# Gate matrices of a dense expert layer as three bf16 products instead of one fp32 product, and 18 more score blocks computed ahead of the expert stream

## The chip, the cores and the metric

The kernel runs as one program on one core of a Trainium2 chip. The metric is the time of one execution on the device in microseconds (us), the median of the runs. A core has TensorE (PE in the profile; its weight loads are listed as PEld), VectorE (DVE), ScalarE (ACT), GpSimd (POOL), SyncE (SP, which here only issues transfers), and 16 DMA engines.

## The reference, cut to what matters

Two transformer blocks follow one another on 512 tokens of width 1024. Each ends in a mixture of 16384 single-row experts, and only that part is touched. For a token, 8 heads choose 16 experts each, which makes 128 slots of an expert number and a gate.

```python
e   = e1 * 128 + e2                 # [tokens, 8, 16] expert numbers
g   = softmax(top)                  # gates
act = gelu(einsum('thkd,td->thk', u_tab[e], x))
y   = einsum('thk,thkd->td', g * act, v_tab[e])
```

## The kernel before, in words

`peer` is called once in each block. It treats tokens in two ways. For 128 of the 512 tokens it gathers the chosen rows of both tables by indirect DMAs (the events `g_u`, `g_v`). For the other 384 tokens (NDT) it computes densely: all 16384 experts are taken as 128 blocks of 128, and block e has three parts.

- **The score block** (`emit_A`): `a_dma` loads 512 KB of the first table (tile `ur`, line 1094); `a_hi` rounds it on ACT (`uh`, line 1099); `a_lo` takes the rest on GpSimd (`ul`, line 1105); `a_mm` makes 24 matmuls of 384 columns (tile `pa`, lines 1112, 1113 and 1115) and a Gelu on ACT into a tile `ga` (line 1117). There are NA = 28 tiles `ga`, and two buffers each of `ur`, `uh` and `ul`.
- **The gates**: for each token a 128 x 128 matrix that holds the gate of expert 128 a + b at [b, a]. The 384 matrices go to DRAM (`Gd`) and come back four expert blocks at a time (`gbuf`, line 1258).
- **The output** (`y`, lines 1293 to 1295): scores times gates (`w`, `wh`, `wl`) with the second table's block (`vr`, `vh`, `vl`), 18 matmuls of 512 columns into six accumulators.

The order of a call is as follows. **Routing** finds experts and gates (written out by hand, with score blocks 0 to 18 between its steps). Then comes the **gate loop**: 12 groups (`tg`) of 32 tokens, each in four steps of 8 tokens. A step makes the one-hot rows `oh2` of the second index on DVE (line 1198) and `oh1`, the one-hot rows of the first index times the gate, on GpSimd or for every fourth step on DVE (line 1200). PE makes one fp32 product for each token (line 1206), whose two operands are read at a stride of 8 elements of 4 bytes; the trace lists each such product as two loads and two matmuls. ACT copies four tokens at a time out of PSUM (`stg`, line 1208), and SP writes each group to `Gd`. `run_ahead` puts three score blocks ahead of the loop, one behind each of the groups in RG, and the rest up to 28 behind the loop. Then comes the **stream** over the 128 blocks: block e makes the output of e and the score block of e + NA, and spreads the gather events evenly over the blocks up to 99.

Outside of the routing and of GpSimd's work in the stream the scheduler of the language sets the order of instructions on each engine; each engine then works in that order, and so does SP's queue of transfers.

## Time and profile before

| what | us |
|---|---|
| median of 3 runs | 4092.33 |
| lowest and highest run | 4079.37, 4106.96 |
| span of the profiled execution | 4090.4 |
| gate loop, first block of the model | 752.6 to 954.4 |
| stream, first block of the model: first and last output matmul | 970.6 to 1959.9 |
| gate loop, second block | 2899.5 to 3100.2 |
| stream, second block | 3116.4 to 4081.1 |

The median lies 1.9 us above the profiled span. The two gate loops and the two streams make up most of the program. A row of a table by stretches gives for each engine its busy time and, after an x, its number of instructions. PE's matmuls overlap, so the pace of matmuls is read from start to start, or from the length of a row of many, and not from the duration of one.

### The profile page before, as it was taken

What the parts mean: (1) busy time and instruction counts of PE and PEld (TensorE: products, weight loads), DVE (VectorE), ACT (ScalarE), POOL (GpSimd) and SP (SyncE); (2) the same over time, 40 slices, a digit from 0 to 9 for tenths busy, and PEclk for the clock granted to TensorE, in tenths of its full rate; (3) what the DMA queues carried; (4) which work ended last, traced back from release to release, by engine and by line L of the source; (5) the groups of instructions that cost most, each with busy time, mean ns of one, the idle gap of its engine ahead of it and who ended that gap; (6) DMA issues with size and microseconds to landing.
All of it is one profiled execution on the core that took longest, in us unless ns stands there. A gap on an engine that the chain in (4) does not pass through costs nothing. (4 is left out here: it accounts for less than half of the span.)

```text
span 4090.4 us, 53234 instructions
## 1 busy us (share of the span) xinstructions
PE 3876.8 (95%) x19062; PEld 3370.2 (82%) x19062; DVE 3004.6 (73%) x5440; ACT 1654.8 (40%) x2567; POOL 2145.8 (52%) x1353
## 2 busy tenths in 40 slices
...
GB/s 112 99 111 106 52 113 79 101 134 230 302 319 320 315 311 315 318 275 221 90 81 57 93 75 100 102 114 79 98 134 250 299 322 314 311 306 308 299 254 150
DMA packets 330057, 784.31 MB, mean 192 GB/s; under 512 B 32048, under 2 KB 148864, under 8 KB 326400
## 3 DMA queue, kind: packets, MB, share of 16 engines
...
q14 instruction: 115, 0.94, 0.1%
...
## 5 line engine op out<-in xcount | busy, mean ns | idle before, releaser
L1105 POOL TENSOR_TENSOR ul<-ur,uh 128x1024 fp32r<-128x1024 f32 x256 | 676.5, 2643 | 378.0 <-ACT uh L1099 259.5
L1112 PE MATMUL pa<-phi,uh 128*128 128x384 f32 x2048 | 695.5, 340 | 0.8 <-ACT ga L1117 0.8
L1113 PE MATMUL pa<-plo,uh 128*128 128x384 f32 x2048 | 694.8, 339 | 0.0
L1294 PE MATMUL y<-vl,wh 128*128 128x512 f32 x1536 | 606.2, 395 | 26.1 <-DVE vl L1263 22.4
L1295 PE MATMUL y<-vh,wl 128*128 128x512 f32 x1536 | 609.2, 397 | 11.3 <-DVE wl L1269 11.3
L1293 PE MATMUL y<-vh,wh 128*128 128x512 f32 x1536 | 603.8, 394 | 1.3 <-ACT wh L1268 1.2
L1243 DVE SCALAR_TENSOR_TENSOR acc<-vrow,act,acc 128x1024 f32<-128x1024 f32 x256 | 392.3, 1532 | 196.6 <-DMA vrow<-in_expert_v_dram,ei 99.5
L1230 DVE SCALAR_TENSOR_TENSOR urow<-urow,hgat 128x1024 f32<-128x1024 f32 x256 | 392.0, 1534 | 172.0 <-DMA urow<-in_peer_u_dram,ei 85.5
L1268 ACT CAST wh<-w 128x384 fp32r<-128x384 f32 x256 | 131.2, 513 | 736.0 <-PE y L1294 483.8
L1099 ACT CAST uh<-ur 128x1024 fp32r<-128x1024 f32 x256 | 269.3, 1052 | 382.9 <-PE pa L1113 149.2
L1115 PE MATMUL pa<-phi,ul 128*128 128x384 f32 x2048 | 402.5, 339 | 18.0 <-POOL ul L1105 17.9
L1112 PEld LDWEIGHTS pa<-phi,uh 128*128 128x128 f32 x2048 | 389.0, 190 | 10.0 <-ACT ga L1117 1.1
L1113 PEld LDWEIGHTS pa<-plo,uh 128*128 128x128 f32 x2048 | 389.1, 190 | 9.6
L1263 DVE TENSOR_TENSOR vl<-vr,vh 128x1024 fp32r<-128x1024 f32 x236 | 353.4, 1498 | 34.6 <-DMA ur<-in_peer_uT_dram 16.2
L1115 PEld LDWEIGHTS pa<-phi,ul 128*128 128x128 f32 x2048 | 362.0, 190 | 19.9 <-POOL ul L1105 19.9
L1206 PE MATMUL pgg<-oh,oh 128*128 128x128 f32 x1536 | 374.3, 421 | 4.4 <-DVE oh L1198 3.9
L1206 PEld LDWEIGHTS pgg<-oh,oh 128*128 128x128 f32 x1536 | 369.9, 337 | 7.1 <-issue 5.3
L1294 PEld LDWEIGHTS y<-vl,wh 128*128 128x128 f32 x1536 | 290.5, 189 | 93.5 <-DVE vl L1263 32.3
L1295 PEld LDWEIGHTS y<-vh,wl 128*128 128x128 f32 x1536 | 290.5, 189 | 85.0 <-DVE wl L1269 22.5
L1293 PEld LDWEIGHTS y<-vh,wh 128*128 128x128 f32 x1536 | 290.8, 189 | 55.5 <-ACT wh L1268 1.7
L77 DVE TENSOR_TENSOR wl<-wr,wh 128x512 fp32r<-128x512 f32 (+1 forms) x276 | 198.9, 729 | 148.9 <-ACT wh L76 148.8
L1200 POOL TENSOR_TENSOR oh<-oha,ohb 128x1024 f32<-128x1024 f32 x72 | 218.2, 3033 | 143.9 <-PE pgg L1206 104.5
...
## 6 DMA issues: line engine op xcount, KB each, us to landing
vr<-in_peer_v_dram SPq DMA_DIRECT2D x128, 512.0 KB
ur<-in_peer_uT_dram SPq DMA_DIRECT2D x128, 512.0 KB
vr<-in_expert_v_dram SPq DMA_DIRECT2D x128, 512.0 KB
ur<-in_expert_uT_dram SPq DMA_DIRECT2D x128, 512.0 KB
...
wr<-in_w_in_dram SPq DMA_DIRECT2D x104, 256.0 KB
...
```

The costliest lines, as they stand in the source:

```text
L1099: A.copy(out=uh, in_=ua[e])
L1105: G.tensor_tensor(out=ul, in0=raw, in1=uh.bitcast(F32), op=OP.subtract)
L1112: T.matmul(pa, uh[:, k, :], hi[:, k, 0:NDT], start=(k == 0), stop=False)
L1113: T.matmul(pa, uh[:, k, :], lo[:, k, 0:NDT], start=False, stop=False)
L1115: T.matmul(pa, ul[:, k, :], hi[:, k, 0:NDT], start=False, stop=(k == 7))
L1206: T.matmul(pg[:, j, :], oh2[:, :, 4 * q + j], oh1[:, :, 4 * q + j], start=True, stop=True)
L1230: V.scalar_tensor_tensor(out=row, in0=row, scalar=1.0, in1=hg_, op0=OP.mult, op1=OP.mult, accum_out=act[:, k:k + 1])
L1243: V.scalar_tensor_tensor(out=acc, in0=vrow.pop(k - 2), scalar=act[:, k - 2:k - 1], in1=acc, op0=OP.mult, op1=OP.add)
L1263: (G if side and EV <= e < EW else V).tensor_tensor(out=vl, in0=vr, in1=vh.bitcast(F32), op=OP.subtract)
L1293: T.matmul(y[t][c], wh[:, ts], vh[:, cs_], start=(e_ == 0), stop=False)
L1294: T.matmul(y[t][c], wh[:, ts], vl[:, cs_], start=False, stop=False)
L1295: T.matmul(y[t][c], wl[:, ts], vh[:, cs_], start=False, stop=(e_ == 127))
```

## The change: what it does, and the diff

In the gate loop the gate is split into three bf16 parts whose sum is the fp32 gate. `oh2` becomes a contiguous bf16 row of 128 for each token, made by eight small DVE comparisons a step. The first index is no longer taken apart: one comparison of 1024 elements gives its one-hot rows (tile `oh12`), and three multiplications give the rows times each part. These tiles are laid out so that a token's operand is 64 pairs of neighbouring bf16 numbers. PE makes three products for each token, each with a weight load of its own. GpSimd has no work left in the loop.

NA goes from 28 to 30. Of the later score blocks every sixth (35, 41, ... 125: 16 blocks) is also computed in the gate loop: its `ga` is written to DRAM (`gad`, 196.6 KB) by SP and read back in the stream, where the score block is then left out. The list `todo` has 27 blocks: three stand ahead of the loop, 24 in it, two a group. For them `a_lo` runs on DVE instead of GpSimd. The diff, without removed comments and docstrings:

```diff
-    O1 = 3
...
-    GM = 4
-    GR = 3
     TB = 3
-    NA = 28
+    NA = 30
...
     TG = 32
+    TK = 8
+    RP = 2
+    SP = 6
     NTG = NDT // TG
...
-        def a_lo(e):
+        def a_lo(e, eng=G):
             raw, uh = ua[e]
             ul = ub.tile([128, 8, 128], F32R, name="ul", tag="ul")
-            G.tensor_tensor(out=ul, in0=raw, in1=uh.bitcast(F32), op=OP.subtract)
+            eng.tensor_tensor(out=ul, in0=raw, in1=uh.bitcast(F32), op=OP.subtract)
             ua[e] = (uh, ul)
-        def a_mm(e):
+        def a_mm(e, keep=None):
             uh, ul = ua.pop(e)
             pa = psA.tile([128, NDT], F32, name="pa", tag="pa")
             for k in range(8):
                 T.matmul(pa, uh[:, k, :], lo[:, k, 0:NDT], start=False, stop=False)
             for k in range(8):
                 T.matmul(pa, ul[:, k, :], hi[:, k, 0:NDT], start=False, stop=(k == 7))
-            ga = ub.tile([128, NDT], F32, name="ga", tag="ga", bufs=NA)
+            ga = keep.tile([128, NDT], F32, name="gs", tag="gs") if keep else ub.tile([128, NDT], F32, name="ga", tag="ga", bufs=NA)
             A.activation(out=ga, in_=pa, func=AF.Gelu)
-            gas[e] = ga
-
-        def emit_A(e):
+            if keep:
+                S.dma_start(out=gad[e], in_=ga)
+            else:
+                gas[e] = ga
+
+        def emit_A(e, eng=G, keep=None):
             a_dma(e)
             a_hi(e)
-            a_lo(e)
-            a_mm(e)
+            a_lo(e, eng)
+            a_mm(e, keep)
         gas = {}
...
-        def run_ahead(n):
-            for e in range(len(gas), min(NA, len(gas) + n)):
-                emit_A(e)
-
-        E = rr.tile([128, 4, 128], F32, name="E")
+        gad = {e: dram.tile([128, NDT], F32, name=f"gad{nm}{e}") for e in range(NA + SP - 1, 128, SP)}
+        todo = list(range(16 + TA, NA)) + list(gad)
+        def run_ahead(n, keep):
+            for _ in range(min(n, len(todo))):
+                e = todo.pop(0)
+                emit_A(e, V, keep if e in gad else None)
         rwx = ExitStack()
         rw = rwx.enter_context(tc.tile_pool(name=nm + "rw", bufs=2))
+        E = rw.tile([128, 4, 128], F32, name="E", bufs=1)
...
+        V.tensor_copy(out=ei, in_=E)
         rwx.close()
         qpx.close()
         rp = ExitStack()
         r1 = rp.enter_context(tc.tile_pool(name=nm + "r1", bufs=1))
-        V.tensor_copy(out=ei, in_=E)
-        iota = r1.tile([128, 128], F32, name="iota")
-        S.dma_start(out=iota, in_=I["k_iota"])
+        s2 = r1.tile([128, NDT], F32, name="s2")
+        io2 = r1.tile([128, 128], BF16, name="io2")
+        sD = [r1.tile([128, NDT * RP], BF16, name=f"sD{j}") for j in range(4)]
         ix = ExitStack()
         ixp = ix.enter_context(tc.tile_pool(name=nm + "ix", bufs=1))
-        i1 = ixp.tile([128, 3, ND, 128], I32, name="i1")
-        f12 = ixp.tile([128, 3, ND, 128], F32, name="f12")
-        V.tensor_scalar(out=i1[:, 0], in0=ei[:, 0:ND, :], scalar1=11, scalar2=None, op0=OP.logical_shift_right)
-        V.tensor_scalar(out=i1[:, 1], in0=ei[:, 0:ND, :], scalar1=7, scalar2=15, op0=OP.logical_shift_right, op1=OP.bitwise_and)
-        V.tensor_scalar(out=i1[:, 2], in0=ei[:, 0:ND, :], scalar1=127, scalar2=None, op0=OP.bitwise_and)
-        sT = [r1.tile([128, NDT], F32 if j == 3 else BF16, name=f"sT{j}") for j in range(4)]
-        for j in range(4):
-            if j < 3:
+        iota = ixp.tile([128, 128], F32, name="iota")
+        S.dma_start(out=iota, in_=I["k_iota"])
+        i1 = ixp.tile([128, 2, ND, 128], I32, name="i1")
+        f12 = ixp.tile([128, 2, ND, 128], F32, name="f12")
+        V.tensor_scalar(out=i1[:, 0], in0=ei[:, 0:ND, :], scalar1=7, scalar2=None, op0=OP.logical_shift_right)
+        V.tensor_scalar(out=i1[:, 1], in0=ei[:, 0:ND, :], scalar1=127, scalar2=None, op0=OP.bitwise_and)
+        def spread(j, src):
+            A.copy(out=sD[j].rearrange("p (t r) -> p t r", r=RP), in_=src.unsqueeze(2).broadcast_to([128, NDT, RP]))
+        for j in range(3):
+            if j < 2:
                 A.copy(out=f12[:, j], in_=i1[:, j])
             pt = (pst, pss)[j // 2].tile([128, 4, 128], F32, name="ptE", tag=("tr", "sc")[j // 2])
             for t in range(ND):
-                T.transpose(pt[:, t, :], GT[:, t, :] if j == 3 else f12[:, j, t, :], ident)
-            A.copy(out=sT[j], in_=pt[:, 0:ND, :].rearrange("p a b -> p (a b)"))
+                T.transpose(pt[:, t, :], GT[:, t, :] if j == 2 else f12[:, j, t, :], ident)
+            pf = pt[:, 0:ND, :].rearrange("p a b -> p (a b)")
+            if j == 0:
+                spread(0, pf)
+                continue
+            if j == 1:
+                A.copy(out=s2, in_=pf)
+                continue
+            for i in range(3):
+                part = ixp.tile([128, NDT], BF16, name=f"gpart{i}")
+                V.tensor_copy(out=part, in_=pf)
+                if i < 2:
+                    rest = ixp.tile([128, NDT], F32, name=f"grest{i}")
+                    V.tensor_tensor(out=rest, in0=pf, in1=part, op=OP.subtract)
+                    pf = rest
+                spread(1 + i, part)
+        irep = r1.tile([128, 128 // RP, TK * RP], BF16, name="irep")
+        V.tensor_copy(out=irep.rearrange("p g (t i) -> p g t i", i=RP),
+                      in_=iota.rearrange("p (g i) -> p g i", i=RP).unsqueeze(2).broadcast_to([128, 128 // RP, TK, RP]))
+        V.tensor_copy(out=io2, in_=iota)
         ix.close()
-        run_ahead(TB)
+        gsp = rp.enter_context(tc.tile_pool(name=nm + "gs", bufs=2))
+        run_ahead(TB, gsp)
         rw = rp.enter_context(tc.tile_pool(name=nm + "gg", bufs=2))
-        irep = r1.tile([128, 128, 8], BF16, name="irep")
-        V.tensor_copy(out=irep, in_=iota.unsqueeze(2).broadcast_to([128, 128, 8]))
-        irtg = r1.tile([128, 16, TG], BF16, name="irtg")
-        V.tensor_copy(out=irtg, in_=iota[:, 0:16].unsqueeze(2).broadcast_to([128, 16, TG]))
+        def onehot(name, in0, j, c0, op, o=None):
+            if o is None:
+                o = rw.tile([128, 128 // RP, TK * RP], BF16, name=name, tag=name)
+            V.tensor_tensor(out=o, in0=in0, in1=sD[j][:, c0 * RP:(c0 + TK) * RP].unsqueeze(1).broadcast_to([128, 128 // RP, TK * RP]), op=op)
+            return o
         for tg in range(NTG):
             stg = rw.tile([128, 128, TG], F32, name="stg", tag="stg")
-
-            def row(j, c0, n, m):
-                return sT[j][:, c0:c0 + n].unsqueeze(1).broadcast_to([128, m, n])
-
             c0 = tg * TG
-            oa_ = rw.tile([128, 8, TG], F32, name="oha", tag="oha")
-            V.tensor_tensor(out=oa_, in0=irtg[:, 0:8], in1=row(0, c0, TG, 8), op=OP.is_equal)
-            V.tensor_tensor(out=oa_, in0=oa_, in1=row(3, c0, TG, 8), op=OP.mult)
-            ob_ = rw.tile([128, 16, TG], F32, name="ohb", tag="ohb")
-            V.tensor_tensor(out=ob_, in0=irtg, in1=row(1, c0, TG, 16), op=OP.is_equal)
-            for t8 in range(TG // 8):
-                tk = slice(t8 * 8, t8 * 8 + 8)
-                oh2 = rw.tile([128, 128, 8], F32, name="oh2", tag="oh2")
-                V.tensor_tensor(out=oh2, in0=irep, in1=row(2, c0 + t8 * 8, 8, 128), op=OP.is_equal)
-                oh1 = rw.tile([128, 128, 8], F32, name="oh1", tag="oh1", bufs=O1)
-                (V if (tg * 4 + t8) % GM == GR else G).tensor_tensor(
-                    out=oh1.rearrange("p (a b) t -> p a b t", a=8), in0=oa_[:, :, tk].unsqueeze(2).broadcast_to([128, 8, 16, 8]),
-                    in1=ob_[:, :, tk].unsqueeze(1).broadcast_to([128, 8, 16, 8]), op=OP.mult)
-                for q in range(2):
+            for tk0 in range(0, TG, TK):
+                oh2 = rw.tile([128, TK, 128], BF16, name="oh2", tag="oh2")
+                for i in range(TK):
+                    V.tensor_scalar(out=oh2[:, i], in0=io2, scalar1=s2[:, c0 + tk0 + i:c0 + tk0 + i + 1], scalar2=None, op0=OP.is_equal)
+                eq1 = onehot("oh12", irep, 0, c0 + tk0, OP.is_equal)
+                oh1 = [onehot(f"oh1{j}", eq1, 1 + j, c0 + tk0, OP.mult, eq1 if j == 2 else None) for j in range(3)]
+                for q in range(TK // 4):
                     pg = psm.tile([128, 4, 128], F32, name="pgg", tag="mm")
-                    for j in range(4):
-                        T.matmul(pg[:, j, :], oh2[:, :, 4 * q + j], oh1[:, :, 4 * q + j], start=True, stop=True)
-                    ts = t8 * 8 + 4 * q
+                    for i in range(4):
+                        for j in range(3):
+                            T.matmul(pg[:, i, :], oh2[:, 4 * q + i], oh1[j][:, :, (4 * q + i) * RP:(4 * q + i + 1) * RP], start=(j == 0), stop=(j == 2))
+                    ts = tk0 + 4 * q
                     A.copy(out=stg[:, :, ts:ts + 4].rearrange("p e t -> p t e"), in_=pg)
             S.dma_start(out=Gd[0][:, tg], in_=stg[:, 0:G0])
             S.dma_start(out=Gd[1][:, tg], in_=stg[:, G0:])
-            if tg in RG:
-                run_ahead(1)
+            run_ahead(-(-len(todo) // (NTG - tg)), gsp)
+        rp.close()
         vrs = {e: load_v(e) for e in range(2)}
-        rp.close()
         pctx.close()
-        run_ahead(NA)
...
             with tc.manual_schedule(engines={mybir.EngineType.Pool}):
-                if e + NA < 128:
+                if e + NA in gad:
+                    gas[e + NA] = ub.tile([128, NDT], F32, name="ga", tag="ga", bufs=NA)
+                    S.dma_start(out=gas[e + NA], in_=gad[e + NA])
+                elif e + NA < 128:
                     emit_A(e + NA)
```

How the rows stand now: first PE at the start of the gate loop, where `pgg` is the gate matrix in PSUM, `pa` a score block, and the operands of `pgg` are the moving and the stationary one. Before:

```order
L1115 MATMUL pa_7174<-phi_4498,ul_7172 128x384 x8
L1206 MATMUL pgg_7218<-oh1_7216,oh2_7214 128x128 x4
L1206 MATMUL pgg_7224<-oh1_7216,oh2_7214 128x128 x4
L1206 MATMUL pgg_7234<-oh1_7232,oh2_7230 128x128 x4
L1206 MATMUL pgg_7240<-oh1_7232,oh2_7230 128x128 x4
```

and now:

```order
L1115 MATMUL pa_7203<-phi_4498,ul_7201 128x384 x8
L1228 LDWEIGHTS oh2_7234
L1228 MATMUL pgg_7250<-oh10_7245,oh2_7234 128x128
L1228 LDWEIGHTS oh2_7234
L1228 MATMUL pgg_7264<-oh10_7245,oh2_7234 128x128
L1112 MATMUL pa_7418<-phi_4498,uh_7414 128x384
L1113 MATMUL pa_7418<-plo_4499,uh_7414 128x384
L1228 LDWEIGHTS oh2_7234
L1228 MATMUL pgg_7250<-oh11_7247,oh2_7234 128x128
```

Eight products a step became 24 pairs of load and product, and the matmuls of a score block stand among them.

Then DVE in the same place. Before, one step after another:

```order
L1198 TENSOR_TENSOR oh2_7246<-irep_7204,sT2_7076 128x1024
L1200 TENSOR_TENSOR oh1_7264<-oha_7209,ohb_7212 128x1024
L1198 TENSOR_TENSOR oh2_7262<-irep_7204,sT2_7076 128x1024
L1191 TENSOR_TENSOR oha_7353<-irtg_7206,sT0_7074 128x256
L1198 TENSOR_TENSOR oh2_7286<-irep_7204,sT2_7076 128x1024
```

and now:

```order
L1221 TENSOR_SCALAR oh2_7322<-io2_7081,s2_7080 128x128 x6
L1212 TENSOR_TENSOR oh12_7331<-irep_7124,sD0_7082 128x1024
L1105 TENSOR_TENSOR ul_7449<-ur_7445,uh_7447 128x1024
L1212 TENSOR_TENSOR oh10_7333<-oh12_7331,sD1_7083 128x1024
L1212 TENSOR_TENSOR oh11_7335<-oh12_7331,sD2_7084 128x1024
L1221 TENSOR_SCALAR oh2_7366<-io2_7081,s2_7080 128x128
L1212 TENSOR_TENSOR oh12_7331<-oh12_7331,sD3_7085 128x1024
```

A step has four operations of 1024 and eight of 128, and on every second step a subtraction of a score block stands among them.

Last SP's queue in the stream near the first score block that comes back from DRAM. Before:

```order
L1131 DMA vr_8654<-in_peer_v_dram 128x1024
L1094 DMA ur_8740<-in_peer_uT_dram 128x1024
L1131 DMA vr_8726<-in_peer_v_dram 128x1024
L1094 DMA ur_8815<-in_peer_uT_dram 128x1024
L1131 DMA vr_8801<-in_peer_v_dram 128x1024
```

and now:

```order
L1094 DMA ur_10780<-in_peer_uT_dram 128x1024
L1134 DMA vr_10690<-in_peer_v_dram 128x1024
L1293 DMA ga_10588<-gad135_4924 128x384
L1094 DMA ur_10852<-in_peer_uT_dram 128x1024
L1278 DMA gbuf_11029<-Gd11_4810 128x12x128
```

The load of `ga` stands behind a load of the second table and ahead of the next load of the first one.

## Rows read from the trace of the kernel before

**Rows 1.** The page: span, then busy us (share) xinstructions by engine.

```profile
span 4090.4 us, 53234 instructions
PE 3876.8 (95%) x19062; PEld 3370.2 (82%) x19062; DVE 3004.6 (73%) x5440; ACT 1654.8 (40%) x2567; POOL 2145.8 (52%) x1353
```

**Rows 2.** Stretches: us, busy (x) of PE, PEld, DVE, ACT, POOL; PEclk, DMA share, GB/s.

```profile
752.60:954.40 201.80, 199.29 (x844) 197.70 (x843) 152.92 (x89) 103.55 (x104) 118.65 (x40) 0.98 0.32 128
2899.50:3100.20 200.70, 198.83 (x844) 197.64 (x844) 152.83 (x90) 104.13 (x104) 116.32 (x40) 0.99 0.32 130
955.00:970.00 15.00, 15.00 (x88) 15.00 (x87) 4.15 (x4) 6.90 (x9) 8.50 (x5) 1.00 0.81 279
1400.00:1500.00 100.00, 100.00 (x508) 91.07 (x508) 81.26 (x86) 35.81 (x49) 76.38 (x44) 1.00 0.88 314
```

**Rows 3.** Gate product's tile, first block: duration ns min/median/max, first and last start.

```profile
L1206 PE MATMUL pgg<-oh,oh x768: 415/420/578, 752.8 to 953.8; 128*128 128x128 f32 x192
L1208 ACT COPY stg<-pgg x96: 1012/1026/1136, 754.9 to 954.3; 128x512 f32<-128x512 f32 x96
```

**Rows 4.** Who waited for that tile: us, times.

```profile
  ACT stg L1208: 93.7, 96
  DVE oh L1198: 41.3, 19
```

**Rows 5.** PE by time in the gate loop: start us, us, instruction, xcount.

```profile
893.74 14.07 PE L1206 MATMUL pgg<-oh,oh 128*128 128x128 f32 x58
```

**Rows 6.** PE by time in the routing: score block, contiguous fp32 product of 128.

```profile
606.05 0.34 PE L1113 MATMUL pa<-plo,uh 128*128 128x384 f32 x1
606.22 1.55 PE L1115 MATMUL pa<-phi,ul 128*128 128x384 f32 x8
607.61 1.05 PE L910 MATMUL psc<-keysT,qs 128*128 128x128 f32 x8
```

**Rows 7.** The tile of that contiguous product: duration ns min/median/max, first and last start.

```profile
L910 PE MATMUL psc<-keysT,qs x256: 270/275/422, 537.6 to 2846.7; 128*128 128x128 f32 x128
```

**Rows 8.** PE's weight loads by time, products of only 64 columns.

```profile
2111.06 1.42 PEld L1521 LDWEIGHTS dpo<-va,dpT 128*128 128x128 f32 x12
2112.40 0.19 PEld L119 LDWEIGHTS mm<-wl,phi 128*128 128x128 f32 x1
```

**Rows 9.** DVE by time in the routing: bf16 comparison of 800, then next operation.

```profile
605.02 1.05 DVE L960 TENSOR_TENSOR eq<-crep,fpos 128x800 bf16<-128x800 bf16 x2
605.99 0.48 DVE L919 MAX8 vals<-scs 128x8 f32<-128x128 f32 x2
```

**Rows 10.** DVE by time: a small operation with a constant, then the next.

```profile
2720.05 0.27 DVE L925 FIND_INDEX8 idx<-vals,scs 128x8 uint32<-128x128 f32 x1
2720.25 0.06 DVE L925 MATCH_VALUE_LOAD idx<-vals,scs 128x8 f32 x1
2721.82 0.16 DVE L938 TENSOR_SCALAR fidx<-idx 128x64 f32<-128x64 uint32 x1
2721.92 0.20 DVE L939 CAST fidx<-idx 128x64 f32<-128x64 uint32 x1
```

**Rows 11.** DVE by time in the gate loop: two fp32 operations without GpSimd.

```profile
907.86 1.23 DVE L1198 TENSOR_TENSOR oh<-irep,sT 128x1024 f32<-128x1024 bf16 x1
909.00 1.22 DVE L1200 TENSOR_TENSOR oh<-oha,ohb 128x1024 f32<-128x1024 f32 x1
```

**Rows 12.** Groups of instructions (count, busy us, mean ns): ACT's part of a score block.

```profile
L1099 ACT CAST uh<-ur 128x1024 fp32r<-128x1024 f32 x256 | 269.3, 1052 | 382.9 <-PE pa L1113 149.2 <-DMA ur<-in_expert_uT_dram 89.3 <-DMA ur<-in_peer_uT_dram 76.7
L1117 ACT ACTIVATE ga<-pa 128x384 f32<-128x384 f32 x256 | 125.4, 490 | 175.3 <-PE pa L1115 173.0 <-issue 2.0
```

**Rows 13.** DVE by time between loop and stream, first block.

```profile
969.12 1.38 DVE L1267 TENSOR_TENSOR w<-gbuf,ga 128x384 f32<-128x384 f32 x2 [1.77 <-DMA gbuf<-Gd]
```

**Rows 14.** DVE's waits in the first stream: us in total, times, longest.

```profile
DVE acc L1243 <- DMA vrow<-in_peer_v_dram,ei: 94.8, 38, 6.1
```

**Rows 15.** The waits of SP's queue in the first stream.

```profile
SPq L1131 <- DVE vl L1263: 632.7, 101, 11.0
```

3 lines of the change are left out of this document (removed).

## The prediction

> **What bounds the kernel now.** I read the page's shares first [rows 1]: PE is busy for 95% of the span, no other engine for more than 73%. Time can therefore only come from less PE work, or from PE's few gaps. Then I read the two stages that the change touches in the table by stretches [rows 2]. In the gate loop of the first block PE is busy for 199.3 of 201.8 us, with DMA at a share of 0.32. In a dense piece of the stream PE is busy for 100 of 100 us, DVE for 81, POOL for 76, and the DMA engines have a share of 0.88 at 314 GB/s. PE sets both stages; in the stream DMA comes next, in the gate loop nothing is near.
>
> In the gate loop a token is one fp32 product, which runs as two matmul instructions: 768 for 384 tokens [rows 3]. 58 of them stand in one row of 14.07 us [rows 5]; without the overlap of the last one that is (14.07 - 0.42) / 57 = 0.239 us each, 0.479 us a token, 184 us a block of the model. Three score blocks stand in the same window (844 - 768 = 76 matmuls, [rows 2]). Theirs start (1.55 - 0.34) / 7 = 0.173 us apart [rows 6], so a score block is 24 x 0.173 = 4.15 us and three are 12.5. 184 + 12.5 is 196.5 of the 201.8 us. ACT and DVE wait for these products (93.7 and 41.3 us, [rows 4]), not the other way round. Why the product is dear is in the rows too: a product of the same shape whose operands lie contiguously takes (1.05 - 0.275) / 7 = 0.111 us an instruction [rows 6, 7], less than half.
>
> In the stream 508 matmuls in 100 us [rows 2] at 42 a block (24 + 18) are 8.27 us a block; taking 4.15 off leaves 4.12 us for the output part.
>
> **The change part by part.** The sum is made for one model block and doubled; the second block shows the same loop (200.7 us, [rows 2]).
>
> *Moved score blocks: -79 us.* Before, PE has done 29 score blocks when the first output matmul starts (19 in the routing, three ahead of the loop, three in it, four behind it), and 99 are left for the stream. Now 48 are done (19 + 27, and blocks 30 and 31 behind the loop), and 80 are left. The stream sheds 19 x 4.15 = 79 us of PE work. This alone saves nothing: 24 of them now stand in the loop, where three stood, and are charged there.
>
> *The loop on PE.* A step of 8 tokens has 24 products of one pass, and on average half a score block (24 in 48 steps), 2.08 us. No row has a bf16 product. Bound from below: 0.055 us, half of the contiguous instruction [rows 6, 7], which streams its 128 columns twice. Bound from above: 0.12 us, half of today's strided instruction [rows 5]; the products of 64 columns, which wait for their weight loads, give (1.42 - 0.19) / 11 = 0.112 us a load of 128 fp32 columns [rows 8], and every new product has a load of its own. The weights are now contiguous, the moving operand is read in pairs, and a bf16 column has half of the bytes, so the row that it is nearest to lies between these; I take the middle of 0.055 and 0.112, 0.084 us. A step is then 24 x 0.084 + 2.08 = 4.09 us, the loop's 48 steps 197 us.
>
> On this price the Trainium skill has two rules, both in "TensorE: Matmul & The Clock Gate". Its section on LDWEIGHTS counts columns, not bytes: 128 / 1.2 = 107 ns a load, which agrees with the 0.112 us of [rows 8] and speaks against my middle value; by it a step would be 4.65 us and the loop 223. Its section on the back-to-back issue gap gives about 81 ns for a stream of pairs of load and matmul of 128 columns, which would make 193 us.
>
> *The loop on DVE.* Four operations of 1024 bf16 elements: the routing's bf16 comparison of 800, with the same kind of broadcast, takes (605.99 - 605.02) / 2 = 0.485 us [rows 9], two elements a cycle with a rest of some 0.07; scaled, 0.60 us. Eight comparisons of 128 with a constant: at most 0.20 us (a search over 128 at one element a cycle, 2720.05 to 2720.25), at least 0.06 (the smallest operation there), and I take 0.10, the step from the 64-element operation to the next [rows 10]. Half a subtraction of a score block, 1.14 us alone [rows 11]: 0.57. Sum 2.40 + 0.80 + 0.57 = 3.8 us a step, 181 us; with the upper bound 4.6 us, 219. These use undisturbed prices, since POOL has nothing left in the loop. So DVE is just behind PE, and as each of a step's first products waits for one DVE tile and the tiles have two buffers, I add 5% for the two waiting for each other: 207 us. ACT has two copies (2 x 1.03, [rows 3]) and half of 1.05 + 0.49 [rows 12], 2.8 us a step, and is hidden; it is next if both others fall. So the loop with 24 score blocks takes 207 us, 5 more than today with three.
>
> *The setup.* Transposes, splitting and copies of the gate's parts stand ahead of the loop, beside the 12.5 us of three score blocks as now. DVE's three subtractions are new there. I charge 3 us; PE's three blocks are the cover, and without them some 8 us would show.
>
> *Between loop and stream.* Today 16.8 us pass from the last gate product (953.8, [rows 3]) to the first output matmul (970.6, in the table of stages); the row of w [rows 13] waits for the gates' return from DRAM. PE is filled then, 15.00 of 15.00 us [rows 2], by four score blocks; now it has the two and idles for 8 us. The chain through DRAM is the same, so the time between the two stays; no row shows what PE needs to pick up again, and between 0 and the 8 us of idle I allow 2.
>
> *Transfers in the stream.* A block moves 314 GB/s x 8.27 us = 2.60 MB. One in six now drops 524 KB and reads 197 KB: 6 x 2.60 - 0.33 = 15.3 MB in 5 x 8.27 + 4.12 = 45.5 us, 336 GB/s, a share of 0.94. DVE waits for gathered rows already (94.8 us for those of the second table alone, [rows 14]), and its 6.7 us a block (81 of 100) must fit in 7.6. Bound below: 0, PE stays the bound. Above: 314 GB/s is all there is; then 15.3 MB take 48.7 us, 3.2 more for each of 16 groups, 51 us. I take 12, near the lower end, since a share of 0.88 is not yet full. The load of `ga` waits on SP's queue for `w` of its block; behind it stands the next load of the first table. SP already stands 632.7 us waiting for `vl` of the same blocks [rows 15], so I charge nothing; if that load came late, `uh` and then PE's next score block would wait.
>
> *Sum.* -79 + 5 + 3 + 2 + 12 = -57 us a block, -114 in all. The profiled span would go from 4090.4 to 3976; the median lies 1.9 above its span: **3978 us**.
>
> **The rivals.**
>
> *A. Each product pays its weight load* (0.112 us). The step is 24 x 0.112 + 2.08 = 4.77 us, the loop 229, with 6 for the coupling 235. Against the 207 that is 28 a block: 4034 us. For it: [rows 8]. Against it: half of the bytes.
>
> *B. The short blocks don't get shorter.* If the queue, the gathers or DVE hold every stream block at 8.27 us, a block without its score block saves nothing, and 16 x 4.15 = 66 us stand in the sum in place of the 12: -79 + 5 + 3 + 2 + 66 = -3 a block of the model, 4086 us. For it: the share of 0.88 and the waits of [rows 14]. Against it: PE has no gap in that stretch, so the others have slack.
>
> *C. Loads come cheap* (0.056 us). PE needs 3.42 us a step, 164 in all, and DVE is the bound with 181, 190 with coupling: 17 a block better, 3944 us. The Trainium skill ("TensorE: Matmul & The Clock Gate", the section on weight-path modes) says that weights of 128 columns that are not fp32 can load about twice as fast as measured there; no run shows it.
>
> *D. Slower: DVE doubles.* If the new operations of 1024 run at one element a cycle, they cost 1.14 us like those of [rows 11], a step 4.56 + 0.80 + 0.57 = 5.9 us, the loop 285: 78 a block more than in the sum, 4134 us. It decides from a loop of 264 us (5.5 us a step) on, where the sum is zero. Against it: [rows 9], the same operation and types at two a cycle.
>
> **How the numbers follow.** The forecast as summed 0.50 (its own range, from products of 0.07 to 0.10 us and transfers between 0 and 20 us: 3945 to 4020); A 0.22; B 0.08; C 0.12; D 0.08. The range runs from C without any loss to transfers (3944 - 24 = 3920) to A with 13 us a block more from transfers (4060), and leaves out B and D. About 1%, 41 us, is what a measurement of this kernel can tell from no change. Faster than 4051: the forecast, C, and most of A (0.17), 0.79. Within 1%: the rest of A, B, and 0.01 of D, 0.14. Slower: 0.07.
>
> **What would show it.** In the profile after: the loop's stretch (207 us with 24 score blocks), the pace of `pgg` in a long row (0.084), DVE's rows of 128 (0.10) and 1024 (0.60); blocks in the dense stream 7.6 us apart on average and a share near 0.94; no POOL in the loop. The forecast is wrong if the product's pace is above 0.11, if DVE's step is above 4.5 us, or if PE shows gaps behind the short blocks that outlast 1 us each.

## The result, and the profile after

The changed kernel takes 4293 us (4280.5 to 4302.3) where the kernel before takes 4088 (4079.4 to 4107.0): a ratio of 1.051 (1.047 to 1.054), 5% slower. The forecast was 3978, some 3% faster.

The first starts and the last starts of the gate product's tile and of the output part's tile give the stages of each model block. (The stream's stage runs from the first to the last output matmul. All stage times below are read so.)

| us | before, block 1 / 2 | after, block 1 / 2 | per block | forecast |
|---|---|---|---|---|
| ahead of the loop (its start, or from the stream before it) | 752.8 / 939.6 | 749.2 / 935.8 | -4 | +3 |
| gate loop | 201.0 / 199.9 | 271.3 / 270.2 | +70 | +5 |
| loop to stream | 16.9 / 17.0 | 20.4 / 21.9 | +4 | +2 |
| stream | 989.4 / 964.5 | 1026.4 / 995.7 | +34 | -67 |

The four come to 107 and 103 us, 210 in both, which is the difference of the two spans (4300.5 - 4090.4). So two stages went wrong, the loop by 65 us a block and the stream by 101.

The page of the changed kernel, with the same columns as [rows 1]:

```profile
span 4300.5 us, 55587 instructions
PE 3884.1 (90%) x19824; PEld 3291.4 (77%) x19824; DVE 3103.6 (72%) x6462; ACT 1655.8 (39%) x2567; POOL 1741.2 (40%) x1227
```

No engine has a larger share of busy time than before, and PE has fallen from 95% to 90%. The table by stretches, columns as in [rows 2]: the gate loop of the first block, the gap behind it, and the dense stream.

```profile
749.20:1020.80 271.60, 257.61 (x1735) 225.37 (x1735) 205.86 (x588) 132.50 (x144) 2.68 (x1) 0.93 0.40 144
1030.00:1041.00 11.00, 0.14 (x1) 0.14 (x1) 4.53 (x6) 3.64 (x5) 8.30 (x6) 0.54 1.04 370
1200.00:1600.00 400.00, 362.37 (x1742) 322.66 (x1742) 298.33 (x313) 125.76 (x172) 253.75 (x157) 0.95 0.82 289
1400.00:1500.00 100.00, 92.44 (x442) 82.59 (x443) 72.66 (x80) 31.55 (x43) 62.09 (x40) 0.95 0.82 291
```

Against [rows 2] every engine and the DMA engines do less in the same 100 us of the stream. Nothing is full there, so the waits have to say what holds the stream.

The gate product in the first loop: its rows by time on PE and DVE (start us, us, instruction, count), and who waited for its tile (us, times).

```profile
799.70 2.51 PE L1228 MATMUL pgg<-oh,oh 128*128 128x128 bf16 x20
802.42 1.29 DVE L1212 TENSOR_TENSOR oh<-oh,sD 128x1024 bf16<-128x1024 bf16 x2
804.39 1.06 DVE L1221 TENSOR_SCALAR oh<-io,s 128x128 bf16<-128x128 bf16 x6
  ACT stg L1230: 84.9, 61
  DVE oh L1221: 62.5, 25
```

Twenty products in 2.51 us, less the 0.297 of the last, are (2.51 - 0.297) / 19 = 0.117 us each, where [rows 5] had 0.239 for half of a token. PE has no gap in this row and the granted clock is 1.00 in it, so a lower clock is not what makes the product dear. DVE's operations of 1024 take 0.6 us as forecast; its small ones take (1.06 - 0.25) / 5 = 0.16, not 0.10.

The waits of the first stream (engine, line, releaser: us, times, longest), the answer to [rows 14] first:

```profile
DVE acc L1263 <- DMA vrow<-in_peer_v_dram,ei: 121.1, 46, 9.5
DVE urow L1250 <- DMA urow<-in_peer_u_dram,ei: 104.0, 41, 9.1
PE y L1317 <- DVE vl L1283: 99.8, 25, 7.3
```

PE waits 99.8 us for `vl`, the low half of the second table's block (10.3 before). A stream block whose score block is not made in the stream is called a short block here, the others long blocks. One such wait, behind a short block, on DVE, POOL and PE (some rows between these are left out):

```profile
1284.91 3.39 DVE L1250 SCALAR_TENSOR_TENSOR urow<-urow,hgat 128x1024 f32<-128x1024 f32 x1 [0.95 <-DMA urow<-in_peer_u_dram,ei]
1291.04 3.40 DVE L1263 SCALAR_TENSOR_TENSOR acc<-vrow,act,acc 128x1024 f32<-128x1024 f32 x1
1294.37 1.21 DVE L1250 SCALAR_TENSOR_TENSOR urow<-urow,hgat 128x1024 f32<-128x1024 f32 x1
1295.98 1.21 DVE L1283 TENSOR_TENSOR vl<-vr,vh 128x1024 fp32r<-128x1024 f32 x1
1284.78 2.42 POOL L1105 TENSOR_TENSOR ul<-ur,uh 128x1024 fp32r<-128x1024 f32 x1
1290.81 2.56 POOL L1105 TENSOR_TENSOR ul<-ur,uh 128x1024 fp32r<-128x1024 f32 x1
1297.25 0.80 PE L1317 MATMUL y<-vl,wh 128*128 128x512 f32 x1 [3.94 <-DVE vl L1283]
1297.84 0.63 PE L1318 MATMUL y<-vh,wl 128*128 128x512 f32 x1
1298.27 0.63 PE L1316 MATMUL y<-vh,wh 128*128 128x512 f32 x1
```

`vl` stands in DVE's queue behind operations on gathered rows; two of them take 3.4 us instead of 1.2, each while POOL makes an `ul`. PE idles 3.94 us, about the 4.1 that the short block saved, and its next matmuls start 0.43 us apart instead of 0.23: the granted clock is at the lower of its two levels (1.2 of 2.4 GHz; 0.50 of full) until 1300.4. From 1190 to 1780 us such a wait comes once in six blocks, behind the short one: the next ends at 1350.69 us, 53.4 us after this one, where six long blocks took 6 x 8.27 = 49.6 us before. So a short block saves 4.15 us of PE's work and loses nearly 8 behind it, through PE's idle time (37.6 of the 400 us from 1200 on) and through its lower clock (0.95 in them).

### The profile page after: what moved, and what is told of

Its sections match the earlier page's. It is cut to its first block, busy times and chain, and to the rows that moved or that the text cites. A ratio compares the mean times of both kernels' runs of the same rounds, so it can differ in the third digit from the quotient of the medians.

```text
span 4300.5 us, 55587 instructions
## 1 busy us (share of the span) xinstructions
PE 3884.1 (90%) x19824; PEld 3291.4 (77%) x19824; DVE 3103.6 (72%) x6462; ACT 1655.8 (39%) x2567; POOL 1741.2 (40%) x1227
## 5 line engine op out<-in xcount | busy, mean ns | idle before, releaser
L1105 POOL TENSOR_TENSOR ul<-ur,uh 128x1024 fp32r<-128x1024 f32 x202 | 517.5, 2562 | 1101.0 <-ACT uh L1099 1030.2
L1317 PE MATMUL y<-vl,wh 128*128 128x512 f32 x1536 | 639.5, 416 | 189.9 <-DVE vl L1283 189.2
L1316 PE MATMUL y<-vh,wh 128*128 128x512 f32 x1536 | 627.2, 409 | 27.7 <-ACT wh L1288 27.7
L1318 PE MATMUL y<-vh,wl 128*128 128x512 f32 x1536 | 632.2, 412 | 7.9 <-DVE wl L1289 7.9
L1263 DVE SCALAR_TENSOR_TENSOR acc<-vrow,act,acc 128x1024 f32<-128x1024 f32 x256 | 420.7, 1643 | 231.6 <-DMA vrow<-in_peer_v_dram,ei 121.1
L1115 PE MATMUL pa<-phi,ul 128*128 128x384 f32 x2048 | 437.3, 351 | 18.8 <-POOL ul L1105 18.4
L1318 PEld LDWEIGHTS y<-vh,wl 128*128 128x128 f32 x1536 | 307.7, 200 | 83.7 <-DVE wl L1289 16.7
L1228 PE MATMUL pgg<-oh,oh 128*128 128x128 bf16 x2304 | 322.9, 295 | 15.4 <-DVE oh L1212 11.2
L1228 PEld LDWEIGHTS <-oh 128*128 128x128 bf16 x2304 | 240.2, 113 | 72.3 <-issue 46.0
L1282 ACT CAST vh<-vr 128x1024 fp32r<-128x1024 f32 x256 | 267.6, 1046 | 37.7 <-DMA vr<-in_peer_v_dram 14.9
```

Source lines behind the costliest of these rows:

```text
L1105: eng.tensor_tensor(out=ul, in0=raw, in1=uh.bitcast(F32), op=OP.subtract)
L1115: T.matmul(pa, ul[:, k, :], hi[:, k, 0:NDT], start=False, stop=(k == 7))
L1228: T.matmul(pg[:, i, :], oh2[:, 4 * q + i], oh1[j][:, :, (4 * q + i) * RP:(4 * q + i + 1) * RP], start=(j == 0), stop=(j == 2))
L1263: V.scalar_tensor_tensor(out=acc, in0=vrow.pop(k - 2), scalar=act[:, k - 2:k - 1], in1=acc, op0=OP.mult, op1=OP.add)
L1316: T.matmul(y[t][c], wh[:, ts], vh[:, cs_], start=(e_ == 0), stop=False)
L1317: T.matmul(y[t][c], wh[:, ts], vl[:, cs_], start=False, stop=False)
```

## The experiments

All runs, each against the kernel before on the same chip. Loop and streams in us, of block 1 / 2.

| run | loop | stream | whole | ratio to before |
|---|---|---|---|---|
| before | 201 / 200 | 989 / 965 | 4088 | 1 |
| after | 271 / 270 | 1026 / 996 | 4293 | 1.051 (1.047 to 1.054) |
| e1_no_short | 244 / 249 | 972 / 966 | 4158 | 1.019 (1.015 to 1.023) |
| e2_last16 | 271 / 272 | 953 / 923 | 4155 | 1.017 (1.013 to 1.022) |
| e3_no_readback | 271 / 272 | 1034 / 996 | 4293 | 1.051 (1.047 to 1.056) |
| e4_gather_first | 271 / 272 | 1033 / 1009 | 4322 | 1.060 (1.055 to 1.064) |
| e5_three_buffers | 221 / 222 | 982 / 959 | 4113 | 1.007 (1.004 to 1.010) |
| e6_pool_low_half | 217 / 216 | 982 / 951 | 4099 | 1.004 (1.002 to 1.006) |
| e7_half_vector | 272 / 272 | 995 / 967 | 4247 | 1.039 (1.036 to 1.042) |
| e8_half_gather | 271 / 272 | 1036 / 1009 | 4323 | 1.059 (1.056 to 1.062) |
| e9_product_price | 221 / 239 | 1008 / 1004 | 4208 | one run |
| e10_no_row_wait | 271 / 272 | 974 / 952 | 4200 | 1.028 (1.023 to 1.033) |
| e11_no_gathers | 274 / 274 | 874 / 861 | 4012 | 0.982 (0.977 to 0.987) |
| e12_one_onehot | 217 / 215 | 974 / 964 | 4102 | 1.004 (1.003 to 1.006) |
| e13_stream_low_on_vector | 272 / 271 | 1049 / 1030 | 4371 | 1.070 (1.067 to 1.073) |
| e14_four_side_by_side | 222 / 222 | 1031 / 985 | 4201 | 1.029 (1.025 to 1.032) |
| e15_all_three | 204 / 203 | 1074 / 1046 | 4265 | 1.042 (1.039 to 1.046) |
| e16_vector_order | 273 / 270 | 978 / 938 | 4193 | 1.027 (1.024 to 1.030) |
| e17_fours_last20 | 208 / 207 | 943 / 919 | 4008 | 0.982 (0.979 to 0.984) |
| e18_fours_last20_order | 207 / 207 | 988 / 952 | 4095 | 1.003 (1.001 to 1.005) |

### The stream: the short blocks, or what they bring along

Without short blocks:

```diff
-gad = {e: ... for e in range(NA + SP - 1, 128, SP)}
+gad = {e: ... for e in ()}
```

> The changed kernel, with the list of the 16 blocks that wait in DRAM made empty: those blocks are computed in the stream again, the bf16 gate loop and the 30 held blocks stay. It has 11 score blocks ahead instead of 27 (3 of them before the loop, 8 in it), and no short block in the stream before the last 30. Theory T1 (the loop is longer because its product goes at 0.117 us and VectorE and TensorE hand over to each other): VectorE needs about 48 steps x 3.7 us + 8 x 1.14 = 187 us and TensorE 1152 x 0.117 + 8 x 4.15 = 168, so the loop takes 187 to 225 us against 271. Theory T2 (the stream got longer only because every sixth block is short): the stream goes back to the pace of before, 8.3 us a block, with two blocks less: 975 to 990 us for the first model block against 1023. Both together: 4040 to 4125 us. The rival to T2, that the stream got longer by something else that the change brought (30 held blocks, other buffers, another order of the instructions), leaves the stream at 1023 us or more, since 16 score blocks return to it: at least 4150 us.

The streams went back to 972 and 966 us, where the kernel before has 989 and 965; the first lies 3 us below the expected 975 to 990. The short blocks between long ones are the cause. The loop stayed at 244 and 249 us with 16 score blocks (66 us of PE) less in it, more than T1's 187 to 225, and so the whole (4158) missed the expected 4040 to 4125.

The same 16 blocks at the end:

```diff
-gad = {e: ... for e in range(NA + SP - 1, 128, SP)}
+gad = {e: ... for e in range(112, 128)}
```

> The changed kernel, with the 16 blocks that wait in DRAM taken from the end: blocks 112 to 127 in place of 35, 41, ..., 125. The same work in the same loop, the same 16 read-backs, but the stream then has 82 blocks with a score block in one run, and 46 without behind them. T1: loop 271 us as in the changed kernel. T2 (short blocks between long ones break the ring): 82 x 8.3 + 46 x 5.0 us = 911, with the 19 us by which the same count falls short of the stream of before 930 us, against 1023: 93 us less in each model block, 4293 - 186 = 4107 us in all (4080 to 4140). The rival, that the read-back of a block from DRAM holds up the loads behind it on SyncE's queue: the 16 reads cost the same wherever they stand, so the time stays near 4293 us (over 4250).

953 us against 1026, with the same work and the same read-backs: the place of the short blocks is worth 73 us in each model block. 20 us of the expected 93 are missing, and the whole (4155) lies above the expected 4080 to 4140.

Without the read-back:

```diff
-S.dma_start(out=gas[e + NA], in_=gad[e + NA])
+V.memset(gas[e + NA], 0.0)
```

> The changed kernel without the read-back: where a short block's scores were loaded from DRAM, VectorE fills the tile with zeros (16 operations of 128x384 in each model block). This leaves the scores of those 16 blocks out of the result. Everything else, the short blocks' places too, stays. T2 (short blocks break the ring): 4293 us within 30, since the blocks stay short. The rival, that the read-back on SyncE's queue or its transfer is what lengthened the stream (1023 us against 989, where 19 score blocks less would make it some 910): 4293 - 2 x 113 = 4070 us, and at least 4200 if it is half of it.

No change in the whole: the read-back costs no more than 16 fills on DVE. (The tiles are still written to DRAM in the gate loop.)

GpSimd's order:

```diff
-emit_A(e + NA)
 while nev < want:
     f_, k_ = ev[nev]; f_(k_); nev += 1
+emit_A(e + NA)
```

> The changed kernel, with the gathers of a block put ahead of its score block's low half in GpSimd's hand-written order (before: behind it). Same work, same blocks short. T2 in its narrow form (a gather stands in GpSimd's queue behind a low half that waits for ScalarE's high half, VectorE then waits for the gathered row, and the low half of the value rows stands behind that): with the gathers ahead VectorE's wait for the row goes, and the stream of 1023 us falls towards the 930 us of an unbroken one: 4110 to 4230 us in all. If the ring is closed elsewhere (TensorE's own place, the two buffers of the high half), GpSimd's order changes nothing: 4293 us within 30.

No gain: the streams take 7 and 13 us more. My narrow form of T2 falls: it is not the gather's place behind `ul`.

Then the three things that a gathered row brings were taken apart. Half of DVE's work on it (the operation on a row of the second table is cut in the same way):

```diff
-V.scalar_tensor_tensor(out=row, in0=row, ..., in1=hg_, ...)
+V.scalar_tensor_tensor(out=row[:, 0:512], in0=row[:, 0:512], ..., in1=hg_[:, 0:512], ...)
```

> The changed kernel, short blocks at their places, with VectorE's two operations for a gathered row (1.21 and 1.27 us for 1024 elements) cut to the first 512 elements; the gathers themselves stay whole. This leaves half of the sums of the fourth token tile out. VectorE's work in the stream falls by some 256 x 0.6 = 150 us in each model block. Theory V (the stream is longer because VectorE, with 8.0 us of work for a long block, low half's hold included, has no slack at a short block, so that TensorE waits there for the low half of the value rows and then goes at half clock): the stream of 1026 us comes down to 910 to 960, and the whole to 4293 - 2 x (65 to 115) = 4060 to 4160 us. The rival (transfers: at a short block they have to come sooner): the transfers are the same, the stream stays at 1000 to 1030 us, and the whole at 4260 to 4300.

Half of its bytes (for both tables; DVE's operations are then on 64 partitions):

```diff
-G.indirect_dma_start(out=row, ..., ap=ei[:, TL, k:k + 1], ...)
+G.indirect_dma_start(out=row[0:64], ..., ap=ei[0:64, TL, k:k + 1], ...)
```

> The changed kernel, short blocks at their places, with every gather fetching 64 of its 128 rows (and VectorE's two operations on 64 partitions, which takes them as long as 128). This leaves half of the fourth token tile out. The transfers in the stream fall by 256 x 0.26 = 67 MB of some 270 in each model block, VectorE's time not at all. Theory V: the stream stays at 1000 to 1030 us, and the whole at 4260 to 4300 us. The rival (transfers): the stream comes down to 910 to 960 us, and the whole to 4060 to 4160.

No gather and so no wait for it (the same for the second table), and, in the second edit, nothing of it at all:

```diff
-G.indirect_dma_start(out=row, ...)
-V.scalar_tensor_tensor(out=row, in0=row, ...)
+V.scalar_tensor_tensor(out=row, in0=hg_, ...)
```

```diff
+ev = []
 pend = []
```

> The changed kernel, short blocks at their places, without the gathers: GpSimd issues none, and VectorE's two operations for a row run as before, on a row that is always there. This leaves the fourth token tile out. Theory W (VectorE's queue is what closes the ring: an operation that waits for a gathered row stands ahead of the low half of the value rows for which TensorE waits): VectorE loses its waits of 99 us in 400, and the stream of 1026 us falls to 920 to 965, the whole to 4293 - 2 x (60 to 105) = 4080 to 4175 us. The rival (the ring is closed by ScalarE's queue, where the casts for the output part stand ahead of that for the score block, whatever VectorE does): the stream stays over 990 us, the whole over 4220.

> The changed kernel, short blocks at their places, without the gathers and without VectorE's operations on them. This leaves the fourth token tile out. VectorE then has 2.3 us of work of its own for a block, besides the hold by GpSimd's low half. Theory W: TensorE alone is left, 82 x 8.3 + 16 x 4.15 + 30 x 4.15 = 872 us at full clock, with the start and some rest 880 to 920 against 1026, the whole 4293 - 2 x (105 to 145) = 4000 to 4080 us. The rival (ScalarE's queue): the stream stays over 980 us.

Half of the bytes gains nothing (1036 and 1009 us). The DMA engines stayed busy for a share of 0.79 in that run, against 0.82, so it leaves open whether their time counts; e16 below moves 320 GB/s at a share of 0.92, so 0.82 is not their limit. Half of the operations is worth 31 and 28 us, and the gathers with their waits 52 and 44: both less than theory V and W had said. Without either the streams are 874 and 861 us, where the expectation put PE's own work at 872. The stretch of e11:

```profile
1200.00:1600.00 400.00, 400.00 (x2005) 361.24 (x2004) 119.40 (x159) 145.66 (x194) 104.20 (x45) 1.00 0.50 157
```

PE is busy in all 400 us at full clock, with short blocks at every sixth place and ScalarE's casts as they were. So those casts are not a cause of their own, and all of it goes with the gathered rows. Which part of their way costs the time e11 can't say: with the rows go DVE's operations and waits, GpSimd's 157 us of issuing gathers in this stretch, and the few Gelus on ScalarE that wait for them. No run takes GpSimd's issuing away alone. (In e10 DVE was busy for 399.5 of these 400 us: the operations had moved ahead in its order. So that run changed more than the wait.)

POOL's `ul` holds up DVE, as the rows of 3.4 us suggest. This hold, taken away in the stream:

```diff
-emit_A(e + NA)
+emit_A(e + NA, V)
```

> The changed kernel, short blocks at their places, with the low halves of the stream's score blocks made on VectorE (1.22 us for 128x1024 there) in place of GpSimd (2.5 us, in which VectorE's operations are held: 3.4 us where 1.2 are usual). Theory V (VectorE has no slack in the stream: 1.22 + 0.55 + 0.55 us of its own, 2.6 rows x 1.25, and some 2.4 us of hold make 8.0 us for a long block): without the hold a long block costs VectorE 6.8 us, the stream of 1026 us falls to 890 to 950, and the whole to 4293 - 2 x (75 to 135) = 4020 to 4140 us. The rival (no hold, the 3.4 us rows are a matter of the record): VectorE gets 82 x 1.22 = 100 us more to do in each model block, the stream gets longer, and the whole passes 4300 us.

The hold is real. The groups of instructions in 1200 to 1600 us (count, busy us, mean ns, idle ahead), after, then e13:

```profile
L1283 DVE TENSOR_TENSOR vl<-vr,vh 128x1024 fp32r<-128x1024 f32 x45 | 79.0, 1755 | 0.0
L1263 DVE SCALAR_TENSOR_TENSOR acc<-vrow,act,acc 128x1024 f32<-128x1024 f32 x57 | 91.6, 1608 | 58.9 <-DMA vrow<-in_peer_v_dram,ei 58.8
L1250 DVE SCALAR_TENSOR_TENSOR urow<-urow,hgat 128x1024 f32<-128x1024 f32 x58 | 82.1, 1415 | 40.3 <-DMA urow<-in_peer_u_dram,ei 40.2
```

```profile
L1283 DVE TENSOR_TENSOR vl<-vr,vh 128x1024 fp32r<-128x1024 f32 x39 | 47.5, 1219 | 0.0
L1263 DVE SCALAR_TENSOR_TENSOR acc<-vrow,act,acc 128x1024 f32<-128x1024 f32 x75 | 96.2, 1282 | 0.4
L1250 DVE SCALAR_TENSOR_TENSOR urow<-urow,hgat 128x1024 f32<-128x1024 f32 x74 | 90.4, 1221 | 103.0 <-DMA urow<-in_peer_u_dram,ei 102.8
```

`vl` goes from 1.76 to 1.22 us. Yet the streams grew by 23 and 34 us, and theory V falls: taking the hold away is not enough. What it is worth alone this run can't say, since DVE's order changed with it: 149 operations on rows for 39 blocks, 3.8 a block, where the changed kernel had 115 for 45, 2.6. POOL no longer waited for `uh`, its gathers went ahead, and DVE still waited 103 us for rows (99 in the changed kernel) with `vl` behind them. So the last test wrote DVE's order by hand, in each block e:

```diff
+with tc.manual_schedule(engines={Pool, DVE}):
+    ready.append(prep(e + 1))   # w, vl, wl
     emit_A(e + NA)
     ...                         # gathers of block e
+    flush_late(nl)              # DVE on the rows gathered in block e - 1
```

> The changed kernel, short blocks at their places, the same work; only VectorE's order in the stream is written by hand: first the products and low halves of the next block (w, vl, wl of e + 1), then the operations on the rows that were gathered one block ago. In the changed kernel these rows' operations stand ahead of the low half for which TensorE waits, and themselves wait for rows (99 us in 400). Theory W (it is this order that keeps the stream long): the stream is then the larger of TensorE's and VectorE's work, 82 x 8.3 + 46 x 5.6 = 938 us, 905 to 965, and the whole 4293 - 2 x (60 to 120) = 4053 to 4173 us. The rival (VectorE's work itself, whatever its order): the stream stays at 1000 us or more and the whole over 4240.

The stretch, and PE's wait for `vl` in it (us, times, longest), in the changed kernel and here:

```profile
1200.00:1600.00 400.00, 388.93 (x1900) 341.20 (x1899) 334.41 (x344) 131.03 (x187) 282.58 (x171) 1.00 0.92 320
PE y L1317 <- DVE vl L1283: 37.6, 7, 6.7
PE y L1306 <- DVE vl L1295: 4.0, 6, 0.8
```

1900 matmuls in the stretch instead of 1742, a clock of 1.00, and PE's wait for `vl` is nearly gone. The same work in another order gives 49 and 58 us in the two streams. The edit is wider than its cut shows, though: the loads and ScalarE's casts of block e + 1 are written a block ahead too, so what DVE's order gives by itself is not separated from that. POOL's hold is still there (`vl` takes 2.21 us on the mean), so the hold alone does not decide. The second stream met the expected 938; the first, with 978, missed the range, and the whole (4193) missed it by 20.

### The loop: the product's price and the handover

```diff
-oh1[j][:, :, (4 * q + i) * RP:(4 * q + i + 1) * RP]
+oh1[j].rearrange("p g x -> p (g x)")[:, (4 * q + i) * 128:(4 * q + i + 1) * 128]   # block 1
+oh1[j][:, 0:64 // RP, (4 * q + i) * RP:(4 * q + i + 1) * RP]                       # block 2, j = 1, 2
```

> The changed kernel with two other forms of the gate product, one in each model block (both leave the gates wrong; times only). In the first the moving operand's 128 columns lie side by side, in place of pairs 32 bytes apart. In the second the operand lies as in the changed kernel, but the second and third product of a token have 64 columns in place of 128. Theory L (the product's 0.117 us is its weight load, 0.112 us each, which nothing hides): both leave a run of products at 0.117 us each. The rival P (reading pairs from places 32 bytes apart costs): the first falls to 0.056 to 0.09 us, the second stays or falls by a third. The rival C (the columns set it): the second falls to 0.117 x (1 + 0.5 + 0.5)/3 = 0.078 us on the mean.

Rows of 20 products on PE by time, one of each model block:

```profile
798.78 1.29 PE L1229 MATMUL pgg<-oh,oh 128*128 128x128 bf16 x20
3055.08 1.72 PE L1232 MATMUL pgg<-oh,oh 128*128 128x64 bf16 x20
```

Side by side: (1.29 - 0.22) / 19 = 0.056 us. With 64 columns: about (1.72 - 0.22) / 19 = 0.079. The loop fell from 271 to 221 and 239 us. The weights' own loads are in both, so they don't set the price: the reading of pairs does, and with it the number of columns. A form of the same kind that gives the exact result:

```diff
-RP = 2
+RP = 4
```

> The changed kernel with its one-hot tiles laid out in fours instead of pairs: four columns of a token side by side, 64 bytes to the next four, the same values and the same result. The gate loop took 271 us with a product at 0.117 us. Theory P (the product waits for its moving operand, line by line): half the lines, so 0.056 to 0.07 us each; TensorE needs 1152 x 0.06 + 24 x 4.15 = 169 us for the loop, VectorE some 205, and the loop falls to 215 to 240 us: the whole to 4293 - 2 x (31 to 56) = 4180 to 4230 us. The rival L (the weight load): 0.117 us and 4293 us within 15, as before.

```profile
804.01 1.29 PE L1228 MATMUL pgg<-oh,oh 128*128 128x128 bf16 x20
```

0.056 us with fours too, the loop at 222 us, the whole inside its range. Theory P's price holds and L falls; why a pair costs so much no run shows.

The handover was tested on e1's loop, with a third buffer:

```diff
-oh2 = rw.tile([128, TK, 128], BF16, name="oh2", tag="oh2")
+oh2 = rw.tile([128, TK, 128], BF16, name="oh2", tag="oh2", bufs=3)   # the oh1 tiles too
```

> As the run without short blocks (its loops took 244 and 249 us, 4158 us in all), with three buffers in place of two for each of the four one-hot tiles of the gate loop. Theory H (the loop is set by the handover: VectorE, some 187 us of work, waits for a free tile, and TensorE, 168 us of work, waits for the next tile; each by turns, and TensorE at half clock after each wait): a third buffer lets VectorE run ahead, so the loop comes down to VectorE's own work, 187 to 205 us, and the whole to 4158 - 2 x 45 = 4040 to 4090 us. The rival, that VectorE's own pace is the bound (its operations take longer beside the other engines, its waits are only the rest of a step): the loop stays at 235 to 249 us and the whole at 4130 to 4160.

The loop fell by 24 and 27 us. Waits in 760 to 940 us, e1, then e5:

```profile
DVE oh L1221 <- PE pgg L1228: 38.2, 27, 2.5
PE pgg L1228 <- DVE oh L1212: 25.8, 40, 1.4
```

```profile
DVE oh L1221 <- PE pgg L1228: 20.5, 14, 2.7
PE pgg L1228 <- ACT stg L1230: 12.8, 21, 0.9
```

With two buffers both engines waited for each other; with three, PE's wait for DVE is gone. The loop stopped at 221, not at 187 to 205, and the whole (4113) was over the expected 4040 to 4090. (In the changed kernel's own loop PE waited only 4.7 us for DVE in this window; a third buffer with pairs was not run there.)

Then the low halves in the loop on GpSimd as well:

```diff
-emit_A(e, V, keep if e in gad else None)
+emit_A(e, G, keep if e in gad else None)
```

> As the run with three buffers, and the low halves of the score blocks in the gate loop (some 1.2 us each on VectorE, 11 of them in each model block) are made on GpSimd, which has nothing else to do there. Theory H with VectorE as the next bound: the loop falls by about 8 x 1.2 = 10 us more in each model block. The rival, by the row of 3.4 us for a VectorE operation that ran beside GpSimd's low half in the stream (1.2 us alone): each low half on GpSimd holds VectorE for some 2.2 us, and the loop gets 8 us longer instead.

The loop takes 4 and 6 us less, between the two forecasts; the hold is there too (six small DVE operations took 3.17 us beside a POOL low half of 2.70), but costs less than POOL takes over.

And one operation for eight tokens' second one-hot:

```diff
-for i in range(TK):
-    V.tensor_scalar(out=oh2[:, i], in0=io2, scalar1=s2[:, ...], op0=OP.is_equal, ...)
+V.tensor_tensor(out=oh2, in0=irt, in1=s2[:, c0 + tk0:c0 + tk0 + TK]..., op=OP.is_equal)
```

> As the run with three buffers and the low halves on GpSimd (loops 216 us, 4099 us in all), with the second one-hot matrix of eight tokens made by one VectorE operation of 128x1024 (some 0.65 us) in place of eight of 128x128 (0.16 each, 1.3 together). Its columns for a token then lie 16 bytes apart, so TensorE's weights are read so. Theory H with VectorE as the bound of that loop (171.5 of 180 us busy): a step of VectorE falls from 3.7 to 3.1 us, 48 of them by 31 us, the loop to TensorE's 168 to 195 us, and the whole to 4099 - 2 x (20 to 35) = 4030 to 4060 us, some 1% faster than before. The rival: a weight load from places 16 bytes apart takes longer than 0.117 us, and the loop gets longer than 216 us with TensorE busy in all of it.

No gain (4102). DVE was busy for 126 of 170 us, so its price came down as expected, but PE was busy for 158 of these 170 us by then, and 20 products took 2.65 us, 0.124 each.

### Both together

`RP = 4`, `NA = 26`, three buffers, and `emit_A(e + NA, V)` in the stream:

> The changed kernel with the fours, with three buffers for the four one-hot tiles, with the stream's low halves on VectorE, and with 26 held blocks in place of 30 for the room (17 blocks wait in DRAM, 85 long blocks are left in the stream). If the two causes (pairs and handover in the loop, VectorE's hold in the stream) are all there is: loop 200 to 220 us, the 205 of VectorE's own work, stream 900 to 960, the whole 4293 - 2 x (50 to 70) - 2 x (70 to 125) = 3900 to 4055 us, 1 to 4% faster than before. If the stream has another bound (transfers, now needed sooner, or ScalarE's queue) it stays at 980 to 1020 us and the whole at 4100 to 4190.

The loop came to 204 us with DVE busy in 168.2 of 170 us, as expected; with 26 held blocks it has 21 score blocks in it, not 24. The streams (1074 and 1046) were longer than both forecasts, with the signs of e13: in 1200 to 1600 us PE waited 81.8 us for `vl` (69.0 in e13). The version that leaves the stream's engines alone and puts the short blocks at the end:

```diff
-RP = 2; NA = 30; gad: range(NA + SP - 1, 128, SP); one-hot tiles bufs=2
+RP = 4; NA = 26; gad: range(108, 128);             one-hot tiles bufs=3
```

> The gate loop with fours and three buffers (204 us with the same number of score blocks in it), 26 held blocks, and the last 20 blocks, 108 to 127, as those that wait in DRAM; VectorE's and GpSimd's order as in the changed kernel. By the run with the last 16 blocks (4155 us, streams 953 and 923 us, loops 271) the stream is the same, as 82 long blocks are left in it, and the loop 67 us shorter: 4155 - 2 x 67 = 4021 us, 4000 to 4045, 1 to 2% faster than the kernel before. If the shorter loop is given back in the stream (the transfers of the first blocks come sooner), 4060 to 4090.

4008 us, 1.8% faster than the kernel before (1.6 to 2.1), inside the range. The loop takes 208 us with 24 score blocks in it where before it took 201 with three, and the stream is 46 us shorter than before in both blocks. Its stretch and the page's engines:

```profile
1200.00:1600.00 400.00, 397.24 (x1999) 360.06 (x1999) 325.59 (x334) 140.51 (x191) 297.35 (x174) 1.00 0.89 314
PE 3691.7 (92%) x19824; PEld 3118.6 (78%) x19824; DVE 3055.7 (76%) x6462; ACT 1648.2 (41%) x2567; POOL 1765.4 (44%) x1227
```

And this version with e16's edit for VectorE's order:

> The version with fours, three buffers and the last 20 blocks in DRAM (4008 us; streams 943 and 919), with VectorE's order in the stream written by hand as in e16. Theory W: with the rows' operations behind, TensorE's 82 x 8.3 us of long blocks go undisturbed and the 46 short blocks at VectorE's 5 us: 905 to 930 us in both streams, 3960 to 4000 us in all. The rival (where no short block stands between long ones VectorE's order was no burden, and a fixed order brings waits of its own, as the 64 us in 400 for ScalarE's vh in e16): 4005 to 4050 us.

The rival holds, and the loss is larger than its 4005 to 4050: the streams are 45 and 33 us longer. In the dense stretch PE is as busy as in e17 (397.6 of 400 us), so there the order has nothing left to gain; the hand-written order loses late in the stream (PE 152.6 of 200 us against 166.7 from 1720 us on), and why was not tested. This fits order and place being two ways around one cause, and does not prove it.

## Why the prediction was wrong, step by step

**The bound now** held: PE sets both stages of the kernel before. What failed is what I read out of it for the others. "PE has no gap in that stretch, so the others have slack" was my argument against rival B. DVE's slack was an average, 81 of 100 us, in a queue that goes in order: at a short block PE needs the next `vl` 4.1 us after the last instead of 8.3, and it stands behind operations on rows. Two of the prediction's own three signs of being wrong came: a product above 0.11 us, and gaps behind the short blocks of far more than 1 us.

**Moved score blocks, -79.** As PE work the step is right: e11's streams of 874 and 861 us are near the 872 that e11's expectation sums up from it. As time it is the step that failed most: the forecast was a stream 67 us shorter, transfers included, and it grew by 34 us on average, since what PE shed at a short block came back as waits for `vl` (99.8 us in the first stream).

**Transfers in the stream, +12.** The wrong obstacle. The share fell to 0.82 instead of rising to 0.94, half of the gathers' bytes gained nothing, and e16 ran faster at 0.92. PE's waits are for DVE's queue, which I had passed with "its 6.7 us a block (81 of 100) must fit in 7.6". Rival B named "the queue, the gathers or DVE" and so had the place, but as a gain that fails, +54 against the sum; the loss came to 101. About half of it goes away with the order written by hand (e16: 49 and 58 us); for the rest the runs show only that it goes with the gathered rows (e11), and how work, waits and order share it stays open.

**The product, 0.084 us.** It is 0.117, near the upper bound of 0.12 and above the 0.112 to which the middle reached. The bound below, 0.055, was right for operands that lie side by side or in fours (0.056); the bound above, half of the strided fp32 instruction, was nearly the answer, and its reason, the strided reading, was in [rows 5] against [rows 6]. I had written that reason down and then gave the price to the weight load of [rows 8]. Rival A had the right size for the wrong reason: its 0.112 us load does not show in e9 and e14, where load and product together take 0.056. The section on LDWEIGHTS in the Trainium skill ("TensorE: Matmul & The Clock Gate") would charge 107 ns for each; the 0.056 us disagree, and agree with the section on weight-path modes, by which such weights load about twice as fast.

**The loop, 207 us.** 1152 x 0.117 + 24 x 4.15 = 234 for PE, where the forecast had 197: the price explains 37 of the 64 us that were missing (fours gave 49 back). The 37 us from 234 to 271 are PE's waits and the clock, which I had put at 5%, some 10: PE is busy for 257.6 of 271.6 us, so 14 are idle, and the rest goes with a clock of 0.93. A third buffer took 24 to 27 us off e1's loop, and 14 off the loop with fours (e17 against e14, both with 24 score blocks in it). The 204 us of e15, which e17's expectation takes as that of the same number of score blocks, are with 21.

**DVE's step, 3.8 us.** The 1024 operations were right (0.60), the small ones 0.16 for 0.10, eight of them 0.5 us a step. Rival D's mechanism did not occur; that its loop of 285 us is near the 271 is chance.

**Setup +3, transition +2.** They came to -4 and +4, both small. In 1030 to 1041 us PE is busy for 0.14 us, at a clock of 0.54, so it idles longer than the 8 us that I had counted.
